# Where the conv taps, the first pair's values and one eviction stand in a hybrid decoder block

## The chip, the cores and the metric

The kernel runs on one core of one Trainium2 chip. The metric is the device time of one execution in microseconds (us), as a median over several executions. One more execution is recorded by the hardware profiler; every duration below is from that one.

## What is computed

Input and output are 512 tokens of 1024 features in float32. The block is a half feed-forward, then two token mixers side by side (a retention of 8 heads and a causal convolution of 31 taps, each behind its gate), then a second half feed-forward, with layer norms between. The middle part, which the change is about, is in the reference (cut):

```python
proj = h @ w_in + b_in
q, k, v, g, glu_a, glu_b, gate_r, gate_c = jnp.split(proj, SPLIT_POINTS, axis=-1)

q = rotary(q.reshape(bsz, s, RET_HEADS, RET_DK), cos, sin) * (RET_DK ** -0.5)
k = rotary(k.reshape(bsz, s, RET_HEADS, RET_DK), cos, sin)
v = v.reshape(bsz, s, RET_HEADS, RET_DV)
r = retention_chunkwise(q, k, v)
mu = jnp.mean(r, axis=-1, keepdims=True)
var = jnp.mean(jnp.square(r - mu), axis=-1, keepdims=True)
r = ((r - mu) * lax.rsqrt(var + LN_EPS)).reshape(bsz, s, V_W) * ret_gn_g.astype(jnp.float32)
ret_out = (jax.nn.silu(g) * r.astype(h.dtype)) @ w_ret_o

u = glu_a * jax.nn.sigmoid(glu_b)
u = lax.conv_general_dilated(u, conv_k, window_strides=(1,), padding=[(CONV_WIDTH - 1, 0)],
                             dimension_numbers=('NWC', 'WIO', 'NWC'),
                             feature_group_count=CONV_CH) + conv_b
u = jax.nn.silu(layer_norm(u, conv_ln_g, conv_ln_b))
conv_out = u @ w_conv_o

merged = jax.nn.sigmoid(gate_r) * ret_out + jax.nn.sigmoid(gate_c) * conv_out
return merged @ w_out
```

There are 8 heads with q and k of 128 and v of 256 features, 1024 channels of u and 31 taps for each.

## The kernel before, in words

**Arithmetic.** Every float32 operand of a product is split in two: `split` (L64 to L66) rounds it on ScalarE (ACT) to a high part (`whi`, `rh`, `vh`, `ph`: line L65) and takes the rest on VectorE (DVE) as a low part (`wlo`, `rl`, `vl`, `pl`: L66). TensorE (PE) then runs three matmuls for one product (L294, L295, L296, called from `mm3`; L711 in the value stage). So before PE can use a block of weights, the block is loaded by a DMA of queue SP, cast on ACT and subtracted on DVE.

**Stages.** The feed-forward fills 0 to 395 us. The value stage (395 to 475 us) computes v for all heads by a Strassen scheme: four products of sums of blocks per unit. Its order is the order of the program text: `product(...)` issues matmuls into a pair of PSUM banks, `take(...)` (L718) evicts such a pair by DVE into `y` or `z`, `give(...)` (L724) adds two results and stores v to DRAM, `block(u, name)` splits a block of weights, and `do(...)` runs named steps on the inputs (`lo1` is a subtraction into `tl`, L138). A `product` that reuses a pair of banks waits for the `take` before it.

The heads stage (475 to 760 us) is ordered by a scheduler, which keeps to data and buffer dependencies and, where the program pins instructions with `pin`, to their order. For each head: `qk_proj` projects q and k and rotates them (L856 to L860: `rs` and `rc`; then a split into `rh` and `rl`), `scores` multiplies them and applies the mask (`pf`, then `ph` and `pl`), `v_in` loads and splits the values of a pair of heads (`vf`, `vh`, `vl`), `retain` multiplies scores and values and normalizes by groups (`gst`, `gmv`, `grs`, `gnm`, then `rn` on ACT, L945), and `gated` transposes `rn` on PE (L954) and multiplies by the gate. Between them `glu_next` computes one more 128 channels of u (`sgb`, `up`).

**The convolution** runs on DVE as filler. `conv_taps` is a generator per 128 channels: one instruction per tap (L325, L331, 29 times L333), 30 yields and an addition of two accumulators (L335). After each unit of work the program calls `conv_some(n)`, which takes n steps from the list of generators, in program order. In the heads stage n is `TAPS_HEAD` for `qk_proj` and `glu_next`, and half of it, rounded down, for each half of a gate unit; after each of the 8 units of the w_ret stage (760 to 860 us) and after the second and third gate units it is `TAPS_LATE`. What is left is then taken at once by `conv_some(10 ** 6)`. The taps of one channel block are pinned to one another, so DVE takes them in order.

**Behind the convolution** stands its layer norm: PE transposes the 8 channel blocks of `cv` (L1020, 32 transposes into 8 PSUM banks), DVE takes statistics of each bank (`cst`, L1021, BATCH_NORM_STATS2), and the banks are free again when these have been read. The fourth gate unit's projection follows on PE.

**Engines** each take their instructions in the one order that was fixed when the program was built; an instruction that waits for a semaphore holds up those behind it on its engine.

Of the kernel before, what the change touches and what calls it, by code (L numbers as in the profile page):

```python
# [8 lines left out]
F32 = mybir.dt.float32  # L9
F32R = mybir.dt.float32r  # L10
AF = mybir.ActivationFunctionType
ALU = mybir.AluOpType
# [14 lines left out]
ALPHA = 2.0 ** 0.25  # L27
KR = 4
WARM = 18
TAPS_HEAD = 6  # L30
TAPS_LATE = 10
HS = S // 2
KH = KD // 2
N_STD = (2, 3)
# [18 lines left out]
def block_kernel(ctx, tc, ap, out):  # L53
    nc = tc.nc
# [6 lines left out]
    def bank():  # L61
        return psum.tile([P, S], F32, name="ps", tag="ps")

    def split(hi, lo, src):  # L64
        nc.scalar.copy(hi, src)  # L65
        nc.vector.tensor_tensor(lo, src, hi.bitcast(F32), op=ALU.subtract)  # L66

    mm = nc.tensor.matmul
    transpose = nc.tensor.transpose

    pin = tc.keep_in_program_order

    def load_unit(src):
        raw = wpool.tile([P, 2048], F32, name="raw", tag="raw", bufs=2)
        nc.sync.dma_start(raw, src)
        parts = []
        for i in range(2):
            hi = wpool.tile([P, 1024], F32R, name="whi", tag="whi")
            lo = wpool.tile([P, 1024], F32R, name="wlo", tag="wlo")
            split(hi, lo, raw[:, i * 1024:(i + 1) * 1024])  # L80
            parts.append((hi, lo))
        return parts
# [227 lines left out]
    def vcol(i):  # L310
        return vec[:, i:i + 1]
# [6 lines left out]
            mm3(ps[:, c], w[k // per] if per < KD else w, (xh, xl), sl, (slice(None), k, c), k == 0, k == KD - 1)  # L318


    conv_todo = []

    def conv_taps(c, odd, up, i):

        op = nc.vector.tensor_scalar(c, up[:, 0:S], vcol(C_CK + i * TAPS), vcol(C_CB + i), op0=ALU.mult, op1=ALU.add)  # L325
        for t in range(1, TAPS):
            pin(op)
            yield
            x, w, acc = up[:, t:t + S], vcol(C_CK + i * TAPS + t), (c, odd)[t % 2]
            if t == 1:  # L330
                op = nc.vector.tensor_scalar_mul(acc, x, w)  # L331
            else:
                op = nc.vector.scalar_tensor_tensor(acc, x, w, acc, op0=ALU.mult, op1=ALU.add)  # L333
        pin(op)
        pin(nc.vector.tensor_tensor(c, c, odd, op=ALU.add))  # L335
# [310 lines left out]
    with ExitStack() as mix:  # L646
# [4 lines left out]

        def glu(i, pool, ps=None, taps=TAPS_HEAD):

            ps = ps or unit_proj(w_in[U_L + i], taps)
            sgb = pool.tile([P, S], F32, name="sgb", tag="t1", bufs=2)
            nc.scalar.activation(sgb, ps[0], AF.Sigmoid, bias=vcol(C_BIN + T_B + i))
            up = mp.tile([P, PAD + S], F32, name="up", bufs=5)
            nc.gpsimd.memset(up[:, :PAD], 0.0)
            nc.vector.scalar_tensor_tensor(up[:, PAD:], ps[1], vcol(C_BIN + T_A + i), sgb, op0=ALU.add, op1=ALU.mult)
            return up  # L660
# [4 lines left out]
        with tc.tile_pool(name="values", bufs=1, reuse_waits="tile") as vp, tc.manual_schedule():  # L665
# [10 lines left out]
            xs, x_steps = strassen_x(vp, split_parts(None))  # L676
            raw, sums, ready = {}, {}, {}
# [16 lines left out]
            def block(u, name):  # L694
                src = (sums if name[0] == "s" else raw)[u, name]
                ready[u, name] = []
                for c in range(2):
                    hi = wpool.tile([P, 1024], F32R, name="whi", tag="whi")
                    lo = wpool.tile([P, 1024], F32R, name="wlo", tag="wlo")
                    split(hi, lo, src[:, c * 1024:(c + 1) * 1024])  # L700
                    ready[u, name].append((hi, lo))

            def product(ps, w, x, first):
                h_, l_ = x
                for k in range(KH):
                    wh, wl = w[k // 2]
                    csl = slice((k % 2) * 512, (k % 2) * 512 + 512)
                    for st in range(2):
                        ssl = slice(st * P, (st + 1) * P)
                        for n, (a, c) in enumerate(((h_, wh), (h_, wl), (l_, wh))):  # L710
                            mm(ps[st], a[:, k, ssl], c[:, csl], start=(first and k == 0 and n == 0),  # L711
                               stop=(k == KH - 1 and n == 2), skip_group_check=True)

            def take(u, name, ps, row, op):

                t = vp.tile([P, 2, 512], F32, name=name)
                for st in range(2):
                    nc.vector.tensor_tensor(t[:, st], ps[st], bv[u][row], op=op)  # L718
                return t
# [7 lines left out]
            def two(t):  # L727
                return t[:, 0], t[:, 1]

            def do(names):  # L730
                for name in names.split():
                    x_steps[name]()
# [11 lines left out]
            qk0 = [mp.tile([P, PAD + S], F32, name="up", bufs=5)[:, :S] for _ in range(2)]  # L744
# [13 lines left out]
            y = [bank() for _ in range(2)]  # L758
# [4 lines left out]
            add(0, "s2", "s1", "a11")  # L763
            load(1, "a11")
            block(0, "s2")
            do("lo1 lo4")
            give(0, 0, 0, two(z1), w, ALU.add)
            product(y, ready[0, "s3"], xs["t3"], True)
            block(0, "a22")
            y1 = take(0, "y1", y, 1, ALU.add)  # L770
            product(z, ready[0, "s2"], xs["t2"], False)
            block(0, "s1")
            z2 = take(0, "z2", z, 1, ALU.subtract)
# [20 lines left out]
            y1 = take(1, "y1", y, 1, ALU.add)  # L794
# [33 lines left out]
        def gate_unit(i, pool, sc):  # L828
            ps = unit_proj(w_in[U_R + i], TAPS_LATE if i else 0)
            sr = pool.tile([P, S], F32, name="sr", tag="sr", bufs=2)  # L830
# [5 lines left out]
        with tc.tile_pool(name="heads", bufs=1, reuse_waits="tile") as hp_:  # L836
            cs = hp_.tile([P, 2, S], F32, name="cs")
            nc.gpsimd.dma_start(cs, ap["cs"])

            def glu_next(taps=TAPS_HEAD):  # L840
                if len(ups) == KD:
# [5 lines left out]
            def qk_proj(h, ps=None):  # L847

                ps = ps or unit_proj(w_in[U_QK + h], TAPS_HEAD)
                r = []  # L850
                for j, t0 in enumerate((T_Q, T_K)):
                    pj = ps[j]
                    bcol = C_BIN + t0 + h
                    rc = hp_.tile([P, S], F32, name="rc", tag="t1", bufs=2)
                    rs = hp_.tile([P, S], F32, name="rs", tag="t2", bufs=2)
                    nc.scalar.activation(rs[0:64], pj[64:128], AF.Identity, bias=vec[64:128, bcol:bcol + 1])  # L856
                    nc.scalar.activation(rs[64:128], pj[0:64], AF.Identity, bias=vec[0:64, bcol:bcol + 1])
                    nc.vector.scalar_tensor_tensor(rc, pj, vcol(bcol), cs[:, 0, :], op0=ALU.add, op1=ALU.mult)
                    nc.vector.tensor_tensor(rs, rs, cs[:, 1, :], op=ALU.mult)
                    nc.vector.tensor_tensor(rc, rc, rs, op=ALU.add)  # L860
                    rh = hp_.tile([P, S], F32R, name="rh", tag="rh", bufs=2)
                    rl = hp_.tile([P, S], F32R, name="rl", tag="rl", bufs=2)
                    split(rh, rl, rc)
                    r.append((rh, rl))
                return r

            def v_in(hp):

                v = []
                for st in range(ST):  # L870
                    vf = hp_.tile([P, 512], F32, name="vf", bufs=2)
                    nc.sync.dma_start(vf, values[hp, st])
                    vh = hp_.tile([P, 512], F32R, name="vh", tag="vh", bufs=4)
                    vl = hp_.tile([P, 512], F32R, name="vl", tag="vl", bufs=4)
                    split(vh, vl, vf)
                    v.append((vh, vl))
                return v

            def g_parts(h):

                ws = load_unit(w_in[U_G + h])
                for j in range(2):
                    ps = bank()
                    feat_proj(ps, ws[j])
                    conv_some(TAPS_HEAD // 2)
                    g = hp_.tile([P, S], F32, name="g", tag="g", bufs=2)
# [69 lines left out]
                    z.append(tok())  # L956
                    nc.vector.scalar_tensor_tensor(z[i], tp, vcol(C_GN + i), gs[e], op0=ALU.mult, op1=ALU.mult)

            qk = qk_proj(0, qk0)
            glu_next(0)  # L960
            for hp in range(H // 2):
                a, b = 2 * hp, 2 * hp + 1
                pa = scores(a, qk)
                v = v_in(hp)
                qk = qk_proj(b)
                ra = retain(a, pa, v)
                ga = g_unit(a)
                gated(a, ra, ga)
                pb = scores(b, qk)
                if hp < H // 4:  # L970
                    glu_next()
                    rb = retain(b, pb, v)
                    gb = g_unit(b)
                else:
                    parts = g_parts(b)
                    gb = [next(parts)]
                    rb = retain(b, pb, v)
                    gb.append(next(parts))
                gated(b, rb, gb)
                if hp < H // 2 - 1:  # L980
                    qk = qk_proj(b + 1)
                    glu_next()


# [4 lines left out]
        with tc.tile_pool(name="ret", bufs=1) as rp_:  # L989
# [6 lines left out]
            for i in range(KD):  # L996
                ws = load_unit(ap["w_ret"][i])
                ps = bank()
                for k in range(16):
                    sl = (slice(None), slice((k % 8) * P, (k % 8 + 1) * P))  # L1000
                    mm3(ps, ws[k // 8], zp[k], sl, (slice(None), slice(None)), k == 0, k == 15)
                conv_some(TAPS_LATE)
                nc.scalar.copy(rt[i], ps)
# [152 lines left out]
```

## Time and profile before

| | |
|---|---|
| median of three executions | 1394.61 us (1394.26 to 1396.43) |
| the profiled execution | 1396.84 us, of which span 1395.1 us, 1.74 us around it |
| mean granted clock of TensorE | 0.993 |
| PE busy | 1364.8 us, 98% of the span |
| DVE busy | 1040.1 us, 75% |
| ACT busy | 607.8 us, 44% |
| DMA | 159.26 MB, mean 114 GB/s |

The profile gives times in us from the start of the span. PE, DVE, ACT and SP are the engines, SPq is the DMA queue that SP issues to. A row's number in brackets is the idle time of its engine just before, with what ended it. [...] "x21" means that 21 instructions of one kind follow one another, and the duration is that of all of them.

### The profile page before, as it was taken

What the parts mean: (1) busy time and instruction counts of PE and PEld (TensorE: products, weight loads), DVE (VectorE), ACT (ScalarE), POOL (GpSimd) and SP (SyncE); (2) the same over time, 40 slices, a digit from 0 to 9 for tenths busy, and PEclk for the clock granted to TensorE, in tenths of its full rate; (3) what the DMA queues carried; (4) which work ended last, traced back from release to release, by engine and by line L of the source; (5) the groups of instructions that cost most, each with busy time, mean ns of one, the idle gap of its engine ahead of it and who ended that gap; (6) DMA issues with size and microseconds to landing.
All of it is one profiled execution on the core that took longest, in us unless ns stands there. A gap on an engine that the chain in (4) does not pass through costs nothing.

```text
span 1395.1 us, 19328 instructions
## 1 busy us (share of the span) xinstructions
PE 1364.8 (98%) x7926; PEld 1209.7 (87%) x7926; DVE 1040.1 (75%) x1484; ACT 607.8 (44%) x886; POOL 21.2 (2%) x37
## 2 busy tenths in 40 slices
PE   9899999999999899999999999799999999999997
PEld 7899999888988788888888888688889999998886
DVE  7888886335889788878797998764488887884336
ACT  5555555223343444454445422192243555554221
POOL 0000000000000000000000000000000000000000
PEclk9999999999999999999999999899999999999999
DMA  5323232523522633222222224123342322325221
GB/s 186 122 94 119 92 121 103 200 91 121 211 76 106 226 99 120 98 99 99 83 103 87 76 106 151 61 69 118 115 169 74 108 105 101 113 93 209 91 91 61
DMA packets 30618, 159.26 MB, mean 114 GB/s; under 512 B 3392, under 2 KB 3520, under 8 KB 15040
## 3 DMA queue, kind: packets, MB, share of 16 engines
q1 hardware_dynamic: 30384, 157.49, 31.5%
q8 instruction: 62, 1.02, 0.3%
q0 software_dynamic: 144, 0.52, 0.2%
q14 instruction: 28, 0.23, 0.0%
HBM read 147.51 MB, written 10.49 MB: 113 GB/s over the span
## 4 chain that ended last, share of the span: by engine, by line
PE 90%; DVE 7%; DMA 1%; ACT 1%; issue 1%; SPq 0%; POOL 0%; DVEq 0%; ACTq 0%
PE ps L201 26%; PE ps L443 19%; PE ps L294 13%; PE ps L295 13%; PE ps L296 13%; PE ps L711 4%; DVE cv L333 1%; DVE wlo L66 1%; DMA h<-in_xT_dram 1%; DVE wlo L158 1%; DMA vf<-values 1%; PE ps L954 1%; DVE st L127 0%; DVE tl L138 0%; DVE ln_y L412 0%
## 5 line engine op out<-in xcount | busy, mean ns | idle before, releaser
L65 ACT CAST whi<-raw 128x1024 fp32r<-128x1024 f32 x148 | 154.1, 1051 | 227.9 <-PE ps L295 146.5
L66 DVE TENSOR_TENSOR wlo<-raw,whi 128x1024 fp32r<-128x1024 f32 x148 | 179.5, 1220 | 61.4 <-ACT whi L65 61.0
L294 PE MATMUL ps<-xh,whi 128*128 128x512 f32 x512 | 201.4, 393 | 8.8 <-DVE cst L1021 8.8
L296 PE MATMUL ps<-xh,wlo 128*128 128x512 f32 x512 | 200.3, 391 | 0.5 <-DVE wlo L66 0.5
L295 PE MATMUL ps<-xl,whi 128*128 128x512 f32 x512 | 200.4, 391 | 0.0
L333 DVE SCALAR_TENSOR_TENSOR cv<-up,vec,cv 128x512 f32<-128x512 f32 x232 | 160.2, 743 | 0.0
L294 PEld LDWEIGHTS ps<-xh,whi 128*128 128x128 f32 x512 | 96.9, 189 | 28.5 <-DVE cst L1021 9.0
L296 PEld LDWEIGHTS ps<-xh,wlo 128*128 128x128 f32 x512 | 96.7, 189 | 21.0 <-DVE wlo L66 0.9
L295 PEld LDWEIGHTS ps<-xl,whi 128*128 128x128 f32 x512 | 96.9, 189 | 19.2
L443 PE MATMUL ps<-whi,hh 128*128 128x512 f32 x320 | 100.0, 390 | 0.0
L443 PE MATMUL ps<-whi,hl 128*128 128x512 f32 x320 | 99.8, 389 | 0.0
L443 PE MATMUL ps<-wlo,hh 128*128 128x512 f32 x320 | 99.8, 389 | 0.0
L66 DVE TENSOR_TENSOR hl<-h,hh 128x512 fp32r<-128x512 f32 x40 | 27.3, 690 | 96.9 <-ACT hh L65 96.9
L201 PE MATMUL ps<-th,whi 128*128 128x256 f32 x312 | 88.5, 284 | 1.0 <-ACT z L209 1.0
L201 PE MATMUL ps<-xh,wlo 128*128 128x256 f32 x312 | 88.3, 283 | 0.0
L201 PE MATMUL ps<-tl,whi 128*128 128x256 f32 x312 | 88.3, 283 | 0.0
L201 PE MATMUL ps<-xl,whi 128*128 128x256 f32 x312 | 88.3, 283 | 0.0
L201 PE MATMUL ps<-xh,whi 128*128 128x256 f32 x312 | 88.3, 283 | 0.0
L201 PE MATMUL ps<-th,wlo 128*128 128x256 f32 x312 | 88.3, 283 | 0.0
L65 ACT CAST hh<-h 128x512 fp32r<-128x512 f32 x40 | 24.1, 622 | 115.2 <-PE ps L443 115.2
L443 PEld LDWEIGHTS ps<-whi,hl 128*128 128x128 f32 x320 | 60.1, 188 | 12.5
L443 PEld LDWEIGHTS ps<-wlo,hh 128*128 128x128 f32 x320 | 60.1, 188 | 12.4
(244 smaller groups left out, 3395.3 us busy)
## 6 DMA issues: line engine op xcount, KB each, us to landing
raw<-in_w_in_dram SPq DMA_DIRECT2D x36, 1024.0 KB, 4.9
raw<-in_w2gu_dram SPq DMA_DIRECT2D x22, 1024.0 KB, 4.8
raw<-in_w1gu_dram SPq DMA_DIRECT2D x21, 1024.0 KB, 4.8
raw<-in_w1dn_dram SPq DMA_DIRECT2D x11, 1024.0 KB, 4.8
raw<-in_w2dn_dram SPq DMA_DIRECT2D x11, 1024.0 KB, 4.8
raw<-in_w_ret_dram SPq DMA_DIRECT2D x8, 1024.0 KB, 4.8
a<-in_w_in_dram SPq DMA_DIRECT2D x4, 1024.0 KB, 5.2
values<-vo SPq DMA_DIRECT2D x16, 256.0 KB, 2.4
```

The lines of the kernel that those rows point to most:

```text
L65: nc.scalar.copy(hi, src)
L66: nc.vector.tensor_tensor(lo, src, hi.bitcast(F32), op=ALU.subtract)
L158: return lambda: nc.vector.tensor_tensor(lo, src, hi.bitcast(F32), op=ALU.subtract)
L201: mm(ps, a[:, sl], c[:, k, :], start=(first and k == 0 and n == 0), stop=(k == KH - 1 and n == 2), skip_group_check=True)
L294: mm(ps, wh[wsl], xh[xsl], start=first, stop=False)
L295: mm(ps, wh[wsl], xl[xsl], start=False, stop=False)
L296: mm(ps, wl[wsl], xh[xsl], start=False, stop=last)
L333: op = nc.vector.scalar_tensor_tensor(acc, x, w, acc, op0=ALU.mult, op1=ALU.add)
L443: mm(acc[st][hf], x[:, sl], wx[:, hf * 512:(hf + 1) * 512], start=(k == 0 and x is ah and wi == 0), stop=(k == nk - 1 and x is al),)
L711: mm(ps[st], a[:, k, ssl], c[:, csl], start=(first and k == 0 and n == 0), stop=(k == KH - 1 and n == 2), skip_group_check=True)
L954: transpose(tp[:, ib * P:(ib + 1) * P], rn[:, ib, e * P:(e + 1) * P], ident)
```

## The change

Three edits. In the value stage, for the first unit, the eviction `y1` and the product that precedes it move ahead of the split of block `a22` and of a `give`, and the step `lo1` moves behind that `give`. In the heads stage the first pair's two splits of values get an artificial dependency (`behind`, without a semaphore) on the split of the first rotated key, and the very first tap of the convolution one on the low part of that key. And the counts of taps rise from 6 to 7 and from 10 to 11. `split` now returns its two instructions, `qk_proj` the last split beside its result.

```diff
-TAPS_HEAD = 6
-TAPS_LATE = 10
+TAPS_HEAD = 7
+TAPS_LATE = 11
...
+    def behind(ins, first):
+        tc.add_manual_dep(ins.ins, first.ins.name,
+                          mybir.DependencyInfo(mybir.DependencyClass.NoSync, mybir.DependencyReason.DATA), reason="order")
...
         op = nc.vector.tensor_scalar(c, up[:, 0:S], vcol(C_CK + i * TAPS), vcol(C_CB + i), op0=ALU.mult, op1=ALU.add)
+        if conv_after:
+            behind(op, conv_after.pop())
...
             block(0, "s2")
-            do("lo1 lo4")
+            do("lo4")
+            product(y, ready[0, "s3"], xs["t3"], True)
+            y1 = take(0, "y1", y, 1, ALU.add)
+            block(0, "a22")
             give(0, 0, 0, two(z1), w, ALU.add)
-            product(y, ready[0, "s3"], xs["t3"], True)
-            block(0, "a22")
-            y1 = take(0, "y1", y, 1, ALU.add)
+            do("lo1")
             product(z, ready[0, "s2"], xs["t2"], False)
...
-                    split(rh, rl, rc)
+                    last = split(rh, rl, rc)
...
-                return r
+                return r, last
...
-                    split(vh, vl, vf)
+                    ops = split(vh, vl, vf)
+                    if hp == 0:
+                        for op, first in zip(ops, rotated):
+                            behind(op, first)
...
-            qk = qk_proj(0, qk0)
+            qk, rotated = qk_proj(0, qk0)
+            conv_after.append(rotated[1])
```

What this does to the engines' order at the three places, first of the kernel before, then of the changed one (each row is one run of equal instructions with its line; lines of the changed kernel are 4 to 11 higher, and its low parts stand on L65).

DVE in the value stage, around the eviction `y` (number 4222 before, 4207 after) and the low parts `tl`:

```order
L66 TENSOR_TENSOR wlo<-sum,whi 128x1024 x2
L138 TENSOR_TENSOR tl<-st,th 128x1024 x2
L724 TENSOR_TENSOR vo<-z_4142,ps 128x512 x2
L66 TENSOR_TENSOR wlo<-raw,whi 128x1024 x2
L718 TENSOR_TENSOR y_4222<-ps,bv_3957 128x512 x2
L66 TENSOR_TENSOR wlo<-sum,whi 128x1024 x2
```

```order
L65 TENSOR_TENSOR wlo<-sum,whi 128x1024 x2
L142 TENSOR_TENSOR tl<-st,th 128x1024
L724 TENSOR_TENSOR y_4207<-ps,bv_3957 128x512 x2
L65 TENSOR_TENSOR wlo<-raw,whi 128x1024 x2
L730 TENSOR_TENSOR vo<-z_4142,ps 128x512 x2
L142 TENSOR_TENSOR tl<-st,th 128x1024
L65 TENSOR_TENSOR wlo<-sum,whi 128x1024 x2
```

The eviction stood behind six instructions after the pair of `wlo`, and now stands behind one.

ACT at the start of the heads stage, with what each row waits for:

```order
L857 ACTIVATE rs<-up,vec 64x512
L65 CAST whi<-raw 128x1024 [waits DMAHW7_49,DVE_49,PE_49]
L65 CAST vh<-vf 128x512 [waits DMAHW4_49,DMAHW0_49]
L65 CAST vh<-vf 128x512 [waits DMAHW5_49]
L65 CAST rh<-rc 128x512 [waits DVE_49]
L65 CAST whi<-raw 128x1024 [waits PE_49,Activation_49]
L656 ACTIVATE sgb<-ps,vec 128x512 [waits DVE_49]
L65 CAST rh<-rc 128x512 [waits DVE_49]
```

```order
L864 ACTIVATE rs<-up,vec 64x512
L65 CAST whi<-raw 128x1024 [waits DMAHW7_49,DVE_49,PE_49]
L65 CAST rh<-rc 128x512 [waits DVE_49]
L65 CAST whi<-raw 128x1024 [waits PE_49,Activation_49]
L662 ACTIVATE sgb<-ps,vec 128x512 [waits DVE_49]
L65 CAST rh<-rc 128x512 [waits DVE_49]
L65 CAST vh<-vf 128x512 [waits DMAHW4_49,DMAHW0_49]
L65 CAST vh<-vf 128x512 [waits DMAHW5_49]
```

The two casts of values, which wait for DMAs, stood ahead of both casts of rotated operands and now stand behind them; the second `rh` is still behind a cast of weights that waits for PE.

DVE at the end of the convolution, up to the first statistics:

```order
L1010 TENSOR_TENSOR rt_7188<-rt_7188,sr 128x512
L333 SCALAR_TENSOR_TENSOR cv<-up,vec,cv 128x512 x3
L66 TENSOR_TENSOR wlo<-raw,whi 128x1024 x3
L1010 TENSOR_TENSOR rt_7189<-rt_7189,sr 128x512
L333 SCALAR_TENSOR_TENSOR cv<-up,vec,cv 128x512 x21
L1021 BN_STATS cst<-ps 128x6
L335 TENSOR_TENSOR cv<-cv 128x512
```

```order
L339 SCALAR_TENSOR_TENSOR cv<-up,vec,cv 128x512 x7
L1021 TENSOR_TENSOR rt_7202<-rt_7202,sr 128x512
L339 SCALAR_TENSOR_TENSOR cv<-up,vec,cv 128x512 x3
L65 TENSOR_TENSOR wlo<-raw,whi 128x1024
L341 TENSOR_TENSOR cv<-cv 128x512
L65 TENSOR_TENSOR wlo<-raw,whi 128x1024 x2
L1021 TENSOR_TENSOR rt_7203<-rt_7203,sr 128x512
L1032 BN_STATS cst<-ps 128x6 x3
```

The 21 taps between the last gating and the first statistics are gone from there; they stand earlier, spread over the units. PE has 28 transposes, one matmul and 4 transposes there before, and 32 transposes without a break now.

## Rows read from the trace of the kernel before

**Rows 1.** Waits of PE, 380 to 900 us: who for whom: total, times, longest.

```profile
PE ps L294 <- DVE cst L1021: 8.8, 1, 8.8
PE ps L294 <- ACT rh L65: 4.5, 1, 4.5
```

**Rows 2.** Busy time by stretch: PE, PEld, DVE, ACT, POOL, clock, DMA share, GB/s.

```profile
34.00:50.00 16.00, 12.43 (x97) 11.62 (x97) 12.96 (x16) 9.95 (x17) 0.00 (x0) 1.00 0.25 88
475.00:905.00 430.00, 416.66 (x2005) 351.61 (x2004) 366.99 (x603) 181.25 (x257) 11.61 (x14) 0.98 0.29 103
483.70:486.70 3.00, 0.07 (x1) 0.00 (x0) 1.15 (x2) 2.17 (x4) 0.00 (x0) 1.00 0.09 36
486.70:493.60 6.90, 5.29 (x16) 4.71 (x17) 5.53 (x10) 3.76 (x7) 0.00 (x0) 0.51 0.26 76
883.20:886.10 2.90, 0.00 (x0) 0.00 (x0) 2.90 (x6) 0.00 (x0) 0.00 (x0) 1.00 0.00 0
886.10:896.40 10.30, 4.42 (x12) 3.52 (x13) 10.30 (x20) 0.00 (x0) 0.00 (x0) 0.50 0.00 0
```

**Rows 3.** DVE's timeline in the value stage: start, duration, instruction.

```profile
411.65 2.35 DVE L138 TENSOR_TENSOR tl<-st,th 128x1024 fp32r<-128x1024 f32 x2
...
417.39 1.28 DVE L718 TENSOR_TENSOR y<-ps,bv 128x512 f32<-128x512 f32 x2
```

**Rows 4.** PE's timeline there, around its wait.

```profile
416.93 0.39 PE L711 MATMUL ps<-whi,tl 128*128 128x512 f32 x1
418.22 0.47 PE L711 MATMUL ps<-whi,th 128*128 128x512 f32 x1 [0.91 <-DVE y L718]
```

**Rows 5.** PE's timeline, the last of one set of matmuls in the value stage.

```profile
472.50 0.39 PE L711 MATMUL ps<-whi,xl 128*128 128x512 f32 x1
```

**Rows 6.** ACT's timeline, the cast of weights released by that matmul.

```profile
472.92 1.05 ACT L65 CAST whi<-raw 128x1024 fp32r<-128x1024 f32 x1 [1.67 <-PE ps L711]
```

**Rows 7.** ACT's timeline at the start of the heads stage.

```profile
484.53 1.17 ACT L65 CAST vh<-vf 128x512 fp32r<-128x512 f32 x2 [4.75 <-DMA vf<-values]
...
486.12 1.04 ACT L65 CAST whi<-raw 128x1024 fp32r<-128x1024 f32 x1
...
487.65 0.60 ACT L65 CAST rh<-rc 128x512 fp32r<-128x512 f32 x1
```

**Rows 8.** PE's timeline at the start of the heads stage.

```profile
483.15 0.39 PE L295 MATMUL ps<-xl,whi 128*128 128x512 f32 x1
483.38 0.39 PE L296 MATMUL ps<-xh,wlo 128*128 128x512 f32 x1
488.31 0.80 PE L294 MATMUL ps<-rh 128*128 128x512 f32 x1 [4.54 <-ACT rh L65]
...
494.13 0.39 PE L294 MATMUL ps<-xh,whi 128*128 128x512 f32 x1
```

**Rows 9.** PE's timeline, another head's scores, undisturbed: first score matmul, next unit's first matmul.

```profile
518.97 0.48 PE L294 MATMUL ps<-rh 128*128 128x512 f32 x1
...
520.92 0.44 PE L294 MATMUL ps<-xh,whi 128*128 128x512 f32 x1
```

**Rows 10.** DVE's timeline at the end of the convolution.

```profile
877.33 13.99 DVE L333 SCALAR_TENSOR_TENSOR cv<-up,vec,cv 128x512 f32<-128x512 f32 x21
```

**Rows 11.** PE's timeline behind the convolution: transposes, waiting matmul, tenth matmul.

```profile
879.97 3.22 PE L1020 MATMUL ps<-ident,cv 128*128 128x128 f32 x28
891.99 0.80 PE L294 MATMUL ps<-xh,whi 128*128 128x512 f32 x1 [8.80 <-DVE cst L1021]
...
896.67 0.40 PE L294 MATMUL ps<-xh,whi 128*128 128x512 f32 x1
```

**Rows 12.** ACT's timeline, normalizing the group statistics of one head.

```profile
689.98 1.94 ACT L945 ACTIVATE rn<-ps,gnm,grs 128x256 f32<-128x256 f32 x4 [3.75 <-DVE gnm L942]
```

**Rows 13.** PE's timeline, the transposes of that head.

```profile
691.81 1.03 PE L954 MATMUL ps<-ident,rn 128*128 128x128 f32 x8
```

**Rows 14.** PE's timeline in the feed-forward, a short wait.

```profile
38.26 0.38 PE L201 MATMUL ps<-th,dhi 128*128 128x256 f32 x1 [1.56 <-ACT y L209]
```

More of the change, by code (lines that the diff above doesn't have):

```diff
@@ L64, in split @@
     def split(hi, lo, src):
-        nc.scalar.copy(hi, src)
-        nc.vector.tensor_tensor(lo, src, hi.bitcast(F32), op=ALU.subtract)
+        return nc.scalar.copy(hi, src), nc.vector.tensor_tensor(lo, src, hi.bitcast(F32), op=ALU.subtract)
     mm = nc.tensor.matmul
@@ L318, in feat_proj @@
             mm3(ps[:, c], w[k // per] if per < KD else w, (xh, xl), sl, (slice(None), k, c), k == 0, k == KD - 1)
-    conv_todo = []
+    conv_todo, conv_after = [], []
     def conv_taps(c, odd, up, i):
         op = nc.vector.tensor_scalar(c, up[:, 0:S], vcol(C_CK + i * TAPS), vcol(C_CB + i), op0=ALU.mult, op1=ALU.add)
+        if conv_after:
+            behind(op, conv_after.pop())
         for t in range(1, TAPS):
@@ L964, in block_kernel @@
                 v = v_in(hp)
-                qk = qk_proj(b)
+                qk, _ = qk_proj(b)
                 ra = retain(a, pa, v)
@@ L980, in block_kernel @@
                 if hp < H // 2 - 1:
-                    qk = qk_proj(b + 1)
+                    qk, _ = qk_proj(b + 1)
                     glu_next()
```

## The prediction

> **What bounds the kernel now.** The page's first part has PE busy for 98% of the span, so only what lets PE stand, or lets it run at half clock, can be won. The second view is the list of PE's waits from 380 to 900 us: two large ones, 8.8 us for the statistics `cst` and 4.5 us for a rotated operand `rh` [rows 1]. The third is the busy time by stretch with the granted clock. After PE's last matmul at 483.38 the clock stays at 1.00 until 486.70, and is then 0.51 until 493.60; after the transposes it stays at 1.00 until 886.10, and is then 0.50 until 896.40 [rows 2]. [...] The fourth view is the timelines of the engines that PE waits for.
>
> **The value stage.** PE would go on 0.23 us after the matmul at 416.93 (matmuls of this size follow one another at 0.23 us, as 483.15 and 483.38 show [rows 8]), so at 417.16, and goes on at 418.22, behind the eviction `y` [rows 4]. That one runs at 417.39 [rows 3], behind the six instructions of the order above. Its data are long there: DVE has not idled before it. In the new order one `tl` precedes it, half of the 2.35 us at 411.65 [rows 3], so it can start at about 412.8 and end 1.28 us later, at 414.1. The wait goes, with 418.22 - 417.16 = **1.06 us**. What is now late is the split of `a22` behind it: two subtractions the size of the `tl` pair, 2.35 us, end at about 416.5, before PE needs them after the next product. Bounds: nothing won, or 1.3 us if the first slow matmul behind the wait (0.47 us against 0.39) goes too. I take the wait alone.
>
> **The start of the heads stage.** ACT casts the values at 484.53, having waited 4.75 us for their DMA, and the rotated operands stand behind them [rows 7]. With the ties the casts of values come after both. But the second `rh`, which the first score matmul needs, is still behind a cast of weights, and that waits for PE to have used the buffer, up to its last but one matmul at 483.15. What such a release takes I read from another one: matmul at 472.50 [rows 5], cast at 472.92 [rows 6], 0.42 us. So the cast can start at 483.57. From cast to PE (cast, sigmoid, `rh`, start of the matmul) it took 488.31 - 486.12 = 2.19 us [rows 7, 8], and I let it take that again: PE goes on at 485.76. The wait shrinks from 4.54 to about 2.0 us and does not vanish. It then ends before the clock has fallen: it fell some 3 us after PE's last matmul, in both places [rows 2], and after a wait of 1.56 us in the feed-forward [rows 14] the stretch stays at 1.00 [rows 2]. At full clock a head's scores take 520.92 - 518.97 = 1.95 us [rows 9], and six matmuls of the unit beside them 6 x 0.23 = 1.38. So the matmul that started at 494.13 [rows 8] starts at 485.76 + 3.33 = 489.09, **5.04 us** earlier. Bounds: the wait gone as well, 7.0 us; the wait unchanged, nothing.
>
> The first tap's tie takes six taps out of DVE's way just there; they fall into the later calls. DVE's queue then holds the rotation first. On SP a load of weights now stands between the second and the third value load. That load waits for a low part of weights, and the third value load waits behind it. The cast of these values stands on ACT ahead of the next cast of weights. As no row shows it, I bound it by the wait for values in [rows 7]: below nothing, above 4.75 us. I take nothing, because PE first has the scores and a whole unit of weights to run, and keep the upper end in the range.
>
> **The taps.** Before, the calls take 12 units x 6 and 16 half gate units x 3 in the heads, 120 in all, and 10 x 10 later: 220 of 240 steps (8 generators of 30). The change adds 12 and 10, so 242: nothing is left for the last call. Half of seven is still three, so gate units keep theirs. The 21 taps at 877.33, 13.99 us on DVE [rows 10], leave the place ahead of the first statistics, for which PE waited 8.80 us [rows 11]. PE then runs 32 transposes, 3.22 x 32 / 28 = 3.68 us, from 879.97 to 883.65, finds a bank read by then (DVE has no tap left there), and starts its tenth matmul of the next unit 9 x 0.23 us later, at 885.72 instead of 896.67 [rows 11]: **10.95 us**. Bounds: 8.8 for the wait alone; 11.9 if the transposes also move closer.
>
> What these 22 earlier taps cost: 13.99 / 21 = 0.67 us each on DVE, 14.7 in all, beside work in which DVE is busy 366.99 of 430 us [rows 2]; 13.99 of that moves within the same stretch, so its share does not rise. The cover is PE's own work. It is gone where PE waits for DVE within a unit; there each tap could cost up to 0.67. The tightest place I found is a head whose normalized rows `rn` on ACT end at 689.98 + 1.94 = 691.92 [rows 12], while PE transposes the first of them at 691.81 [rows 13], straight behind other work; the chain to `rn` runs over DVE (`gnm`). I take 0 there, as in this head the new order puts no other instruction ahead of `gnm`, and up to 14.7 for the range's reasoning below.
>
> **Sum:** 1.06 + 5.04 + 10.95 = 17.05 us, against the profiled execution's 1396.84 (span 1395.1 and 1.74 around it), so 1379.8. That execution lies 2.23 above the median of 1394.61; from the median it is **1377.5**.
>
> [...] In the row the clock fell 2.9 us after the 28 transposes and 6.1 us after the last matmul with weights; had transposes counted as idle, it would have fallen some 3 us after 879.97, while the stretch to 886.10 is at 1.00 [rows 2, 11]. So I let 32 transposes keep the clock. [...]
>
> **Rivals.**
> 1. *The clock falls at the heads' start all the same*, because the shorter wait is long enough. For it: two waits of over 4 us did it. Against: the delay of 3 us in both. Price: the slow stretch, (494.13 - 488.31) - 3.33 = 2.49 us [rows 8, 9]. Time 1380.0. [...]
> 2. *The clock falls behind the 32 transposes.* Price: from 891.99 to 896.67 PE took 4.68 us [rows 11] for nine matmuls (2.07) and four transposes (0.46), so 2.15 lost. Time 1379.7.
> 3. *The wait at the heads' start only moves.* `rh` still stands behind a cast that waits for PE and a sigmoid, and the values' loads are later. Then only 1.06 and 10.95 come: 1382.6. For it: no row shows how soon the cast can start; against: both inputs (weights loaded, buffer released at 483.15) are there.
> 4. *The taps come onto the path.* If all 22 cost PE their 0.67 us, 14.7 of the 17.05 go: 1392.2, no measurable change. Against: DVE's idle time of 63 us in that stretch [rows 2].
> 5. *Slower: the heads' statistics come late.* If taps and reordering put `gnm` behind so much that PE waits as it did for `rh`, each such head costs 4.54 of waiting and 2.49 of slow clock, 7.03; three of the eight make 21.1, so 4.0 slower, 1398.7. It decides from a lateness of about 4.7 us (4.54 and the head's small slack); a unit gets one or two more taps, 0.67 to 1.33 us, so the scheduler would have to add over three.
>
> **How the numbers follow.** A measurement of this kernel can tell about 0.2%, 2.8 us, from no change. Chances: forecast 0.68 (with small new waits), rival 1 0.09, rival 2 0.05, rival 3 0.10, rival 4 0.05, rival 5 0.03. Forecast and rivals 1 to 3, and a little of rival 4 (fewer taps on the path), are faster: 0.93; the rest of rival 4 is no change, 0.04; rival 5 is 0.03. The range takes in rivals 1 to 3 above, to 1383.0; below, the wait at the heads' start gone as well (2.0) and the small upper ends: 1375.0.
>
> **What would show it.** Right: PE's list of waits without `cst`, `rh` at about 2 us, no `y`; the clock at 1.00 from 483 to 500 and from 883 to 897; 32 transposes and then matmuls at 0.23; DVE with no long run of taps behind 877. Wrong: a new releaser in that list (`rn`, `vh`, `wlo` of the w_ret stage) of over a microsecond, or a stretch with a clock near 0.5 in the heads.

## The result, and the profile after

The changed kernel takes 1379.79 us (median of four, 1378.51 to 1380.4) against 1395.22 us of the kernel before, timed with it (1394.26 to 1396.43): a ratio of 0.9888, 95% interval 0.9871 to 0.9905, so 15.4 us less. The forecast was 1377.5 in a range of 1375.0 to 1383.0. The profiled execution took 1380.4 us, its span is 1378.6.

PE's waits from 380 to 900 us, the view of [rows 1], now have one row:

```profile
PE ps L298 <- ACT rh L65: 2.1, 1, 2.1
```

The statistics `cst` and the eviction `y` have left the list, and the wait for the rotated operand is 2.1 us, as forecast. But at the heads' start the clock fell all the same. The busy time by stretch, columns as in [rows 2], at the start of the heads and behind the convolution:

```profile
481.70:484.80 3.10, 1.04 (x5) 0.76 (x5) 1.97 (x3) 3.05 (x5) 0.00 (x0) 1.00 0.06 24
484.80:488.20 3.40, 3.40 (x14) 3.01 (x13) 2.33 (x5) 1.16 (x3) 0.00 (x0) 0.51 0.85 301
874.70:878.20 3.50, 3.50 (x34) 3.44 (x32) 2.81 (x6) 1.63 (x2) 0.00 (x0) 1.00 0.00 0
878.20:882.00 3.80, 3.80 (x19) 3.16 (x18) 3.77 (x10) 0.00 (x0) 0.00 (x0) 1.00 0.00 0
```

The third figure from the right, ahead of DMA share and GB/s, is the granted clock as a share of full speed: 0.51 from 484.8 to 488.2, and 1.00 through the 32 transposes and behind them.

**The value stage.** DVE's timeline, to be read beside [rows 3], and PE's at the matmul that waited in [rows 4]:

```profile
410.95 1.22 DVE L142 TENSOR_TENSOR tl<-st,th 128x1024 fp32r<-128x1024 f32 x1
412.09 1.28 DVE L724 TENSOR_TENSOR y<-ps,bv 128x512 f32<-128x512 f32 x2
413.29 2.35 DVE L65 TENSOR_TENSOR wlo<-raw,whi 128x1024 fp32r<-128x1024 f32 x2
```

```profile
416.22 0.39 PE L717 MATMUL ps<-whi,tl 128*128 128x512 f32 x1
416.44 0.39 PE L717 MATMUL ps<-whi,th 128*128 128x512 f32 x1
```

The eviction starts behind one `tl` and is over at 413.37, 3.07 us before the matmul that waited for it (21.76 us after the stage's first, as before without the wait: 394.68 + 21.76 = 416.44), which follows the one ahead of it by 0.22.

**The start of the heads.** ACT's timeline, beside [rows 7], and PE's, beside [rows 8]:

```profile
478.23 0.62 ACT L65 CAST rh<-rc 128x512 fp32r<-128x512 f32 x1
481.75 1.04 ACT L65 CAST whi<-raw 128x1024 fp32r<-128x1024 f32 x1 [2.90 <-PE ps L299]
482.70 0.68 ACT L662 ACTIVATE sgb<-ps,vec 128x512 f32<-128x512 f32 x1
483.28 0.61 ACT L65 CAST rh<-rc 128x512 fp32r<-128x512 f32 x1
483.79 1.14 ACT L65 CAST vh<-vf 128x512 fp32r<-128x512 f32 x2
```

```profile
481.27 0.39 PE L299 MATMUL ps<-xl,whi 128*128 128x512 f32 x1
481.50 0.39 PE L300 MATMUL ps<-xh,wlo 128*128 128x512 f32 x1
483.94 0.50 PE L298 MATMUL ps<-rh 128*128 128x512 f32 x1 [2.06 <-ACT rh L65]
...
488.93 0.40 PE L298 MATMUL ps<-xh,whi 128*128 128x512 f32 x1
```

The first rotated operand is cast at 478.23, early. Then ACT stands for 2.90 us at a cast of weights until PE has come to its last but one matmul (481.27; the cast follows 0.48 later), and runs cast, sigmoid and second `rh`: 483.94 - 481.75 = 2.19 us to PE, the forecast to the hundredth. The seventh matmul of the unit beside the scores, the one that the forecast counted to, starts at 488.93, 4.99 us after PE went on, where 3.33 was forecast.

**Behind the convolution.** DVE's timeline, beside [rows 10], and PE's, beside [rows 11]:

```profile
871.51 0.68 DVE L1021 TENSOR_TENSOR rt<-rt,sr 128x512 f32<-128x512 f32 x1
875.39 1.89 DVE L1032 BATCH_NORM_STATS2 cst<-ps 128x6 f32<-128x512 f32 x3 [3.19 <-PE ps L1031]
```

```profile
874.75 3.65 PE L1031 MATMUL ps<-ident,cv 128*128 128x128 f32 x32
878.16 0.48 PE L298 MATMUL ps<-xh,whi 128*128 128x512 f32 x1
...
880.30 0.39 PE L298 MATMUL ps<-xh,whi 128*128 128x512 f32 x1
```

After the last gating DVE now waits 3.19 us for the transposes, where it had 21 taps to do. PE goes from the last transpose to the next unit without a wait.

### The profile page after: what moved, and what is told of

Read it like the earlier page. It is cut to its first block, busy times and chain, and to the rows that moved or that the text cites. A ratio compares the mean times of both kernels' runs of the same rounds, so it can differ in the third digit from the quotient of the medians.

```text
span 1378.6 us, 19327 instructions
## 1 busy us (share of the span) xinstructions
PE 1361.3 (99%) x7926; PEld 1207.8 (88%) x7926; DVE 1038.3 (75%) x1484; ACT 607.5 (44%) x886; POOL 21.5 (2%) x37
## 4 chain that ended last, share of the span: by engine, by line
PE 93%; DVE 4%; ACT 1%; DMA 1%; issue 0%; SPq 0%; POOL 0%; DVEq 0%; ACTq 0%
PE ps L205 26%; PE ps L449 20%; PE ps L299 14%; PE ps L300 14%; PE ps L298 13%; PE ps L717 6%; DVE wlo L162 1%; DMA h<-in_xT_dram 1%; PE ps L964 1%; DVE ln_y L418 0%; PE ps L430 0%; DVE st L169 0%; DVE tl L142 0%; DVE st L131 0%; DVE clo L162 0%
## 5 line engine op out<-in xcount | busy, mean ns | idle before, releaser
L65 ACT CAST whi<-raw 128x1024 fp32r<-128x1024 f32 x148 | 154.2, 1051 | 223.4 <-PE ps L299 153.9
L65 DVE TENSOR_TENSOR wlo<-raw,whi 128x1024 fp32r<-128x1024 f32 x148 | 179.1, 1221 | 57.9 <-ACT whi L65 57.7
L65 DVE TENSOR_TENSOR hl<-h,hh 128x512 fp32r<-128x512 f32 x40 | 27.3, 689 | 97.0 <-ACT hh L65 97.0
L65 ACT CAST hh<-h 128x512 fp32r<-128x512 f32 x40 | 24.1, 622 | 115.1 <-PE ps L449 115.1
```

What stands on the lines that cost most here:

```text
L65: return nc.scalar.copy(hi, src), nc.vector.tensor_tensor(lo, src, hi.bitcast(F32), op=ALU.subtract)
```

## Where the 15.4 us came from

The two programs have the same matmuls, so the time between two landmarks of PE's timeline can be compared: the value stage's first matmul (395.39 before, 394.68 after), the last matmul ahead of the first scores, the first matmul of the first retention (503.67 and 498.48), the first transpose of the convolution (879.97 and 874.75), the first transpose behind its statistics (905.53 and 889.15), and the end of PE's last matmul. Durations in us, for all runs, each from its one profiled execution:

| kernel | to 395 | values | heads' start | to transposes | behind convolution | behind |
|---|---|---|---|---|---|---|
| before | 395.39 | 87.99 | 20.29 | 376.30 | 25.56 | 481.78 |
| changed | 394.68 | 86.82 | 16.98 | 376.27 | 14.40 | 481.73 |
| taps only | 395.39 | 88.02 | 20.39 | 376.27 | 14.39 | 481.71 |
| ties only | 394.69 | 87.99 | 16.95 | 376.30 | 25.31 | 481.71 |
| eviction only | 395.14 | 86.82 | 20.06 | 376.31 | 25.78 | 481.92 |
| changed, taps 7 and 10 | 395.65 | 86.81 | 16.97 | 376.38 | 15.54 | 481.71 |
| changed, taps 6 and 11 | 394.69 | 86.82 | 16.98 | 376.31 | 18.47 | 481.77 |
| changed, `lo1` back | 394.25 | 86.81 | 16.93 | 376.26 | 14.40 | 481.70 |
| changed, no tap tie | 393.82 | 86.81 | 19.44 | 376.30 | 14.40 | 481.68 |
| changed, no value tie | 394.82 | 86.82 | 19.49 | 376.28 | 14.40 | 481.78 |
| changed, sigmoid behind | 394.22 | 86.81 | 14.87 | 376.29 | 14.40 | 481.68 |
| changed, cast behind | 393.95 | 86.82 | 13.87 | 376.28 | 14.40 | 481.68 |
| changed, both behind | 395.06 | 86.81 | 13.01 | 376.27 | 14.39 | 481.71 |

The changed kernel gains 1.17 in the values, 3.31 at the heads' start, 0.03 in the 376 us of heads and retention product, and 11.16 behind the convolution: 15.67, against 15.4 in the medians. The first column, where nothing was changed, varies from 393.82 to 395.65 between executions; so the spans of two single executions can differ by more than a microsecond that is no one's doing, and terms of this size have to be read between landmarks.

## The experiments

**Each part alone.** The taps only: the kernel before with

```diff
-TAPS_HEAD = 6
-TAPS_LATE = 10
+TAPS_HEAD = 7
+TAPS_LATE = 11
```

> The kernel before with the tap counts 7 and 11 alone. Theory (three terms in series on PE, each its own): the wait for the statistics goes and the stretch behind the 32 transposes stays at full clock, so about 11.2 us less than before (the trace of the changed kernel gained 11.15 there); the waits for y (0.9 us) and for the rotated operand (4.5 us) stay as they are, and in the heads PE loses nothing. Rival (the ties carry part of it: without them the earlier taps stand ahead of the rotation on DVE): the wait for the rotated operand grows over 4.5 us by 0.7 us or more and the gain is under 10 us.

Measured: 1385.36 us, ratio 0.9924 (0.9907 to 0.9941); 11.17 us less behind the convolution, and 0.1 us more at the heads' start. Its waits of PE, 380 to 900 us:

```profile
PE ps L294 <- ACT rh L65: 4.8, 1, 4.8
PE ps L711 <- DVE y L718: 0.9, 1, 0.9
```

The wait for the operand is 0.3 longer than before, less than the 0.7 of a further tap, and the 376 us of the heads are as long as with six taps. The ties carry no part of this term, and the 22 earlier taps cost PE nothing.

The ties only: the change without its other two parts,

```diff
-TAPS_HEAD = 7
-TAPS_LATE = 11
+TAPS_HEAD = 6
+TAPS_LATE = 10
...
-            do("lo4")
-            product(y, ready[0, "s3"], xs["t3"], True)
-            y1 = take(0, "y1", y, 1, ALU.add)
-            block(0, "a22")
+            do("lo1 lo4")
             give(0, 0, 0, two(z1), w, ALU.add)
-            do("lo1")
+            product(y, ready[0, "s3"], xs["t3"], True)
+            block(0, "a22")
+            y1 = take(0, "y1", y, 1, ALU.add)
```

> The kernel before with the two ties alone. Theory: PE's wait for the rotated operand falls from 4.5 to about 2.1 us, the granted clock falls all the same about 1 us after PE has gone on, and the gain is about 3.3 us, not the 5.0 of the prediction. Rival (the clock fell in the changed kernel by chance of that one execution): the stretch from 483 to 490 us stays at 1.00 and the gain is 5.0 us. The wait for the statistics (8.8 us) stays.

Measured: 1391.43 us, ratio 0.9971 (0.9959 to 0.9982); 3.34 us at the heads' start. The wait is 2.1 us, and the busy time by stretch there, from PE's idle time to the unit behind the scores:

```profile
482.90:485.50 2.60, 0.54 (x3) 0.33 (x3) 1.49 (x2) 2.56 (x4) 0.00 (x0) 1.00 0.05 20
485.50:489.00 3.50, 3.50 (x14) 3.20 (x13) 2.03 (x4) 0.92 (x3) 0.00 (x0) 0.51 0.71 250
489.00:492.00 3.00, 3.00 (x15) 2.46 (x15) 3.00 (x8) 1.34 (x4) 0.00 (x0) 1.00 0.38 145
```

The fall is no chance of one execution: the rows show it in the changed kernel (0.51 from 484.8), with the ties only (0.51 from 485.5) and with `lo1` back (0.50 from 483.6, in the last section), and in all five profiled executions with a wait of 2.06 us at this place (these three, 7 and 10, 6 and 11) the heads' start took 16.93 to 16.98 us.

The eviction only: the kernel before with the move in the value stage, as in the diff of the change.

> The kernel before with the move in the value stage alone. Theory: the wait of 0.91 us for y goes, with the start of PE behind it 1.2 us in all, and no other wait of the value stage takes its place; the rest as before. Rival: the split of the next block, now behind the eviction, is late by some tenths and the gain is under 0.6 us.

Measured: 1394.52 us, ratio 0.9991 (0.9982 to 1.0001), which by itself shows nothing; between the landmarks the value stage is 1.17 us shorter, and the wait for `y` is gone from the list:

```profile
PE ps L294 <- DVE cst L1022: 8.8, 1, 8.8
PE ps L294 <- ACT rh L65: 4.0, 1, 4.0
```

The wait for `rh` is half a microsecond shorter than before (4.0 against 4.5) without an edit there: ACT waits 4.23 us for the values' DMA in this execution, against 4.75.

**How much of the tail may stay.** The changed kernel with `TAPS_LATE = 10`:

```diff
-TAPS_LATE = 11
+TAPS_LATE = 10
```

> The changed kernel with 10 instead of 11 taps in the late units, so 232 of 240 steps are taken early and 9 DVE instructions of the convolution are left behind the last gating. Theory (PE waits only for what of the tail outlasts its 28 transposes): the tail ends 9 x 0.667 us after it starts, PE goes on 1.1 us later than with none left, the wait listed for the statistics is about 0.9 us, the clock stays at 1.00, and the kernel is about 1.1 us slower than the changed one. Rival (each tap that is left costs its 0.667 us): 6 us slower. Second rival (the clock falls also here): about 3 us slower.

Measured: 1382.04 us, ratio to before 0.9903 (0.9889 to 0.9918); 1.14 us more behind the convolution than the changed kernel, as expected (the medians are 2.25 us apart; it is the landmarks that carry this). DVE's tail, and PE's wait with the clock behind it:

```profile
873.17 6.05 DVE L339 SCALAR_TENSOR_TENSOR cv<-up,vec,cv 128x512 f32<-128x512 f32 x9
```

```profile
879.88 0.50 PE L298 MATMUL ps<-xh,whi 128*128 128x512 f32 x1 [0.85 <-DVE cst L1032]
879.90:886.00 6.10, 6.10 (x29) 5.08 (x30) 6.10 (x13) 0.08 (x1) 0.00 (x0) 1.00 0.00 0
```

And with 6 and 11:

```diff
-TAPS_HEAD = 7
+TAPS_HEAD = 6
```

> The changed kernel with 6 instead of 7 taps in the heads, so 230 of 240 steps are taken early and 11 DVE instructions of the convolution are left at the end. Theory: two more than the 9 of the run with 7 and 10, so the wait for the statistics is 0.85 + 1.33 = 2.2 us; as the wait of 2.06 at the heads' start brought the clock down, this one does too, for about 1.7 us more: about 4.1 us slower than the changed kernel. Rival (transposes ahead of the wait keep the clock up): the stretch stays at 1.00 and it is 2.5 us slower.

Measured: 1383.93 us, ratio to before 0.9917 (0.9902 to 0.9932); 4.07 us more than the changed kernel in that stage. PE's wait, and the clock ahead of, behind and after it:

```profile
880.19 0.50 PE L298 MATMUL ps<-xh,whi 128*128 128x512 f32 x1 [2.17 <-DVE cst L1032]
```

```profile
878.00:881.20 3.20, 1.03 (x6) 0.83 (x6) 3.20 (x6) 0.00 (x0) 0.00 (x0) 1.00 0.00 0
881.20:884.70 3.50, 3.50 (x12) 2.83 (x11) 3.50 (x10) 0.00 (x0) 0.00 (x0) 0.51 0.00 0
884.70:888.00 3.30, 3.30 (x16) 2.73 (x15) 2.25 (x5) 0.16 (x1) 1.01 (x1) 1.00 0.31 42
```

Two instructions more on DVE are 1.32 us of waiting (2.17 against 0.85) and 1.6 us of slow clock on top. So the price of the tail is not per tap: 0.67 each in waiting from some length on, then a step. By the wait of 0.85 for nine, a tail of about seven would cost nothing; that is an estimate, no run has a tail so short other than none at all. The transposes ahead of the wait of 2.17 us did not keep the clock up here: it was 0.51 from 881.2 to 884.7.

**What the moved `lo1` does.** The changed kernel with both low parts ahead of the eviction again:

```diff
-            do("lo4")
+            do("lo1 lo4")
...
-            do("lo1")
```

> The changed kernel with the step lo1 back at its old place, so that both low parts stand ahead of the eviction on DVE. Theory (the eviction has room to spare): it ends 1.1 us later, at about 414.5 on the changed kernel's clock, still ahead of the matmul that needs it at 417.1, so PE has no wait in the value stage and the stage takes as long. Rival (the order is tight): a wait of 0.2 us or more for y or for the low part of the next block.

Measured, one execution: 1379.94 us; the value stage takes 86.81 us, as with the move. The eviction's place ahead of the block's split and the `give` is what counts, the place of `lo1` is free.

**Which tie does it.** The changed kernel without the values' tie:

```diff
-                    if hp == 0:
-                        for op, first in zip(ops, rotated):
-                            behind(op, first)
```

> The changed kernel without the tie of the values; the tie of the first tap stays. In its order the two casts of values stand ahead of the first rotated operand on ACT again. Theory (what held PE was the values' DMA ahead of the rotation on ACT): the cast of values waits for its DMA, PE waits 4 us or more for the rotated operand and the clock falls: about 3 to 4 us slower than the changed kernel. Rival (taps ahead of the rotation held it): a wait near 2 us, as in the changed kernel.

Measured, one execution: 1383.17 us; the heads' start takes 19.49 us, 2.51 more than with the tie, less than the 3 to 4 expected. ACT's timeline:

```profile
482.21 1.17 ACT L65 CAST vh<-vf 128x512 fp32r<-128x512 f32 x2 [4.28 <-DMA vf<-values]
483.30 0.61 ACT L65 CAST rh<-rc 128x512 fp32r<-128x512 f32 x1
483.81 1.04 ACT L65 CAST whi<-raw 128x1024 fp32r<-128x1024 f32 x1
```

The cast of values waits 4.28 us for its DMA, as in [rows 7], and PE 4.0 us. The DMA came a little earlier than before, so the wait is 0.5 shorter than the 4.5 of [rows 1].

Without the tap's tie:

```diff
-            conv_after.append(rotated[1])
```

> The changed kernel without the tie of the first tap; the tie of the values stays. In its order DVE takes seven taps ahead of the rotation, and on ACT the first rotated operand is cast behind the second cast of weights, which waits for PE. Theory (the wait left at the heads' start is the chain cast of weights, casts and sigmoid on ACT behind PE's release): one cast more stands in that chain, so PE waits about 2.6 us instead of 2.06, the clock falls as before, and the kernel is about 0.6 us slower than the changed one. Rival (the values' tie is all that counts): the same wait of 2.06 and the same time.

Measured: 1382.13 us, ratio to before 0.9906 (0.9891 to 0.992); the heads' start takes 19.44 us, 2.46 more than the changed kernel, where 0.6 was expected. ACT's timeline:

```profile
480.83 1.04 ACT L65 CAST whi<-raw 128x1024 fp32r<-128x1024 f32 x1 [3.39 <-PE ps L299]
481.78 0.61 ACT L65 CAST rh<-rc 128x512 fp32r<-128x512 f32 x1
483.15 0.69 ACT L662 ACTIVATE sgb<-ps,vec 128x512 f32<-128x512 f32 x1 [0.76 <-DVE rl L65]
483.75 0.62 ACT L65 CAST rh<-rc 128x512 fp32r<-128x512 f32 x1
```

One cast more stands behind the cast of weights, as expected, but the sigmoid also waits 0.76 us for the low part `rl` on DVE: the sigmoid's tile is the buffer that the first rotated operand has left only then (both carry the tag `t1`, two buffers). PE waited 3.41 us, and the rest went to the slow clock, 0.50 from 484.0 to 490.1 and so longer than in the changed kernel. So both ties are needed: without either one, 2.5 of the 3.3 us are lost. The values' tie clears ACT's queue, the tap's DVE's, and with it the first operand's place ahead of the weights on ACT.

**What the clock asks, and a better version.** The sigmoid behind the second rotated operand:

```diff
-            nc.scalar.activation(sgb, ps[0], AF.Sigmoid, bias=vcol(C_BIN + T_B + i))
+            op = nc.scalar.activation(sgb, ps[0], AF.Sigmoid, bias=vcol(C_BIN + T_B + i))
+            if sgb_after:
+                behind(op, sgb_after.pop())
...
             conv_after.append(rotated[1])
+            sgb_after.append(rotated[0])
```

> The changed kernel with the sigmoid of the unit before tied behind the second rotated operand on ACT. Theory: the sigmoid's 0.58 us leave the chain, PE waits about 1.5 us instead of 2.06, and as after the waits of 1.36 and 1.56 us in the feed-forward the clock stays at 1.00; 2.2 us less than the changed kernel. Rival (any wait of this size at this place brings the clock down): the clock falls and only 0.6 us are won.

Measured: 1378.11 us, ratio to before 0.9878 (0.9863 to 0.9892); 2.11 us less at the heads' start than the changed kernel. PE's wait, and the stretches ahead of and behind its start:

```profile
482.91 0.50 PE L298 MATMUL ps<-rh 128*128 128x512 f32 x1 [1.49 <-ACT rh L65]
```

```profile
481.20:482.90 1.70, 0.22 (x1) 0.00 (x0) 0.54 (x1) 1.61 (x3) 0.00 (x0) 1.00 0.06 22
482.90:488.00 5.10, 5.09 (x26) 4.34 (x27) 5.10 (x10) 2.63 (x6) 0.00 (x0) 1.00 0.65 214
```

0.57 us less waiting are worth 2.11, since the clock stays at 1.00 until 488.00.

The cast of the first gate unit's second half behind that operand:

```diff
-            split(hi, lo, raw[:, i * 1024:(i + 1) * 1024])
+            ops = split(hi, lo, raw[:, i * 1024:(i + 1) * 1024])
+            if i and cast_after:
+                behind(ops[0], cast_after.pop())
...
+                if hp == 0:
+                    cast_after.append(rotated[0])
                 ga = g_unit(a)
```

> The changed kernel with one tie more: the cast of the second half of the first gate unit's weights, which waits for PE's last but one matmul and which PE needs only a whole unit later, goes behind the second rotated operand. Theory: that operand is ready before PE has finished its unit, the wait at the heads' start is under 0.3 us, the clock stays at 1.00 and the kernel is about 3.7 us faster than the changed one (2.06 of waiting and about 1.7 of slow clock). Rival (the wait only moves, now to the masked scores or the values for the first retention): a wait of over 1 us for ph, vh or vl behind the scores, and a gain under 2 us.

Measured: 1377.44 us, ratio to before 0.9873 (0.9857 to 0.989); 3.11 us less at the heads' start, of 3.7 expected. The wait for `rh` is gone, and a smaller one has come:

```profile
PE ps L304 <- DVE rl L65: 0.6, 1, 0.6
```

```profile
481.26 0.75 DVE L669 SCALAR_TENSOR_TENSOR up<-ps,vec,sgb 128x512 f32<-128x512 f32 x1 [1.48 <-PE ps L304]
481.93 0.68 DVE L65 TENSOR_TENSOR rl<-rc,rh 128x512 fp32r<-128x512 f32 x1
```

The second low part stands on DVE behind the eviction `up`, which waited 1.48 us for PE's last matmul. The rival had a new wait, but at the masked scores and over 1 us; none of them appears.

Both further ties together (the two diffs above):

> The two further ties together: the gate unit's second cast and the sigmoid of the unit before, both behind the second rotated operand. Theory: in the run with the cast alone the second low part of the rotation stood on DVE behind the eviction up, which waits for PE's last matmul, and PE waited 0.60 us for it; with the sigmoid behind, it stands ahead of up, so PE has no wait listed from 380 to 900 us, the clock stays at 1.00 there, and the kernel is about 0.7 us faster than with the cast alone (3.8 faster than the changed one). Rival (the masked scores, whose buffers and mask come late, are next): a new wait of 0.5 us or more behind the scores and no gain over the cast alone.

Measured: 1376.88 us, ratio to before 0.9862 (0.9845 to 0.9878); 0.86 us less at the heads' start than with the cast alone, 3.97 less than the changed kernel. PE has no wait listed between 380 and 900 us, and no slow clock:

```profile
470.00:490.00 20.00, 20.00 (x94) 16.75 (x93) 17.05 (x28) 11.59 (x18) 0.24 (x2) 1.00 0.67 239
490.00:500.00 10.00, 10.00 (x60) 8.88 (x59) 10.00 (x17) 5.41 (x8) 0.00 (x0) 1.00 0.47 158
```

This version is faster than the kernel before. Its lead over the changed one rests on the trace (3.97 us between landmarks) and on medians of 1376.88 and 1379.79, which were timed against the kernel before at different times; the two intervals of their ratios overlap.

## Why the prediction was right, and by how much it was off

- **The value stage**, 1.06 forecast, 1.17 measured. The wait went and nothing took its place. The term left out the slower first matmul behind a wait (0.47 us against 0.39), the upper bound of 1.3 had it.
- **The start of the heads**, 5.04 forecast, 3.31 measured. The queue on ACT was read right: the release (0.48 us, 0.42 forecast), the chain of 2.19 us and the wait of 2.0 (2.06) came as worked out. The step that failed is "It then ends before the clock has fallen". The wait did end before the fall, and the clock fell all the same, at about 484.8, 0.9 us after PE had gone on. The first rival, held at a chance of 0.09, came true here, and so did one of the prediction's own signs of being wrong, a stretch with a clock near 0.5 in the heads. The delay itself came as read: 3.3 us from the start of PE's last matmul (481.50) to the fall, as before (483.38 to 486.70), though with `lo1` back it was 2.5 (481.06 to 483.6). What was wrong is the assumption that a wait must last until the fall to bring it about. The slow clock cost 1.5 us by the run with the sigmoid behind (2.11 less 0.57 of waiting) and 1.7 by the forecast's 3.33, not the rival's 2.49: the stretch at half clock was 3.4 us long here, and 6.9 before, with PE busy for 5.29 of it [rows 2]. The 0.9 us at full clock ahead of it saved nothing: with `lo1` back the clock fell only 0.1 us after PE had gone on, and the heads' start took as long (16.93 us).
- **The taps**, 10.95 forecast, 11.16 measured. The 32 transposes took 878.16 - 874.75 = 3.41 us to the next matmul, not 3.68: dividing the 28 transposes' 3.22 us counts the end of the last one, which overlaps the next (the 32 are listed with 3.65 us, and the next matmul starts 3.41 after the first). The second rival, a clock that falls behind the transposes, did not come: 1.00 through them and behind. So these transposes, which the profile lists as matmuls with `ident`, did not act on the clock as standing did: they took 3.41 us, longer than the 2.06 us of standing behind which the clock fell at the heads' start, and it stayed at 1.00. The run with 6 and 11 taps agrees: the clock fell only 6.4 us after the first transpose (881.2 - 874.8), and 1.0 us after PE had gone on from its wait; after PE's last matmul at the heads' start it fell 2.5 us later with `lo1` back, 2.8 with the ties only (482.68 to 485.5) and 3.3 in the changed kernel, and with 6 and 11 it was still at 1.00 after 3.79 (481.51 to 485.30).
- **What the earlier taps cost**: nothing, as taken. The 376 us from the first retention to the transposes are the same to 0.12 us in all runs, with six taps or with seven.
- **The third rival** (the wait only moves) and **the fourth and fifth** (taps on the path, late statistics) did not come.
- **The value loads** behind the load of weights on SP cost nothing that shows: no wait of PE for `vh` or `vl` is listed.
- **The sum**: 17.05 forecast, 15.67 between the landmarks and 15.4 in the medians. The 1.4 too much are the 1.73 of the heads' start, nearly all of it the slow clock, less the 0.3 too little in the two other terms. The mechanism held in two terms of three; the range held the time because it took in the first rival.

## What to carry to other kernels

When a wait is only shortened, read what the remaining wait does to the clock as a step, not as a length. Here, against the version without any wait there, one of 1.49 us made the stage 1.86 us longer and one of 2.06 made it 3.97 longer. In an engine's queue ask of each instruction ahead of the awaited one what it waits for itself: casts that wait for a DMA, or for the very engine that stands waiting, belong behind. And filler work may end a little late where other work covers it: against the changed kernel nine taps left cost 1.14 us, eleven 4.07, and the 21 of the kernel before 11.16.

## What was not expected of the hardware

Behind waits of 2.06 and 2.17 us the clock fell only after the wait had ended, with PE busy again. After the wait of 2.17 us behind the transposes PE went on at 880.19; the clock was 1.00 until about 881.2 and then 0.51 for 3.5 us, with PE busy for all of the 3.5. After the same wait of 2.06 us at the heads' start the time from PE's going on to the fall differed from run to run: 0.9 us in the changed kernel, 0.1 with `lo1` back (the first two rows), and over 1.3 with 6 and 11 taps, where PE went on at 483.95 (the third row):

```profile
483.51 0.73 PE L298 MATMUL ps<-rh 128*128 128x512 f32 x1 [2.06 <-ACT rh L65]
483.60:487.00 3.40, 3.40 (x11) 3.02 (x12) 1.66 (x4) 0.90 (x2) 0.00 (x0) 0.50 0.68 217
484.00:485.30 1.30, 1.30 (x7) 1.20 (x8) 1.30 (x3) 0.94 (x2) 0.00 (x0) 1.00 0.19 32
```

The heads' start took the same 16.93 to 16.98 us in all of them. What sets this time, the runs do not show. After waits of 0.85 us (7 and 10), 1.49 (sigmoid behind) and 1.56 ([rows 14], the first row of [rows 2]) the clock stayed at 1.00 throughout. Between 1.56 and 2.06 nothing was tried.
